# A decoder layer with two branches: another order of work in its first block

## The chip, the core and the metric

The kernel runs on one core of one Trainium2 chip. The metric is device time in microseconds (us), from the first to the last instruction of the program, as the median of several runs. TensorE (PE, with its weight loads as PEld) multiplies matrices into PSUM; VectorE (DVE), ScalarE (ACT) and GpSimd (POOL) work element by element; SyncE (SP) and ScalarE issue the transfers between HBM and SBUF.

## What is computed

One layer of a decoder over 16 meta tokens and 2048 tokens of 1024 channels. An input projection of the normalised input `u` feeds two branches, an SSD scan with a short convolution and a gated linear attention (GLA); their outputs are merged by sigmoid gates, projected, added to the input and normalised. Cut to what matters here:

```python
def hybrid_layer(hres, ...):
    u = rmsnorm(hres, norm_w)
    proj = jnp.einsum('bld,dn->bln', u, w_in)
    z, xbc, dt_raw, q, k, v, g_gla, a_lr, merge_g = split_cols(proj, IN_WIDTHS)
    xbc = jax.nn.silu(causal_depthwise_conv(xbc, conv_w, conv_b))
    ...
    dt = jax.nn.softplus((dt_raw + dt_bias).astype(jnp.float32))
    a = -jnp.exp(a_log.astype(jnp.float32))
    y_m, s_m = ssd_chunked(xs[:, :m], dt[:, :m], a, bm[:, :m], cm[:, :m], N_META, s0)
    y_r, _ = ssd_chunked(xs[:, m:], dt[:, m:], a, bm[:, m:], cm[:, m:], SSD_CHUNK, s_m)
    y = jnp.concatenate([y_m, y_r], axis=1) + d_skip[:, None] * xs
    y_ssd = rmsnorm_in_groups(y * jax.nn.silu(z), ssd_norm_w)
    gate_logit = jnp.einsum('blr,rk->blk', a_lr, gla_gate_w2) + gla_gate_b
    log_a = (jax.nn.log_sigmoid(gate_logit.astype(jnp.float32)) / GLA_GATE_TEMP)
    ... # GLA with q, k, v and the running sums of log_a; y_gla
    gates = jax.nn.sigmoid(merge_g)
    return hres + merged(gates, y_ssd, y_gla) @ w_out
```

## The kernel before

The 2048 tokens are four blocks of 512; block 0 also carries the 16 meta tokens (`m0` is 16 there and 0 elsewhere). Every product is made of three matmuls on TensorE, since each operand is split into a high half, rounded to the fast type, and a low half, the rest (`accum`, L209 to L211: high by high, high by low, low by high). The split of a weight is a copy on ScalarE and a subtraction on GpSimd (L171, L172); that of `u` a copy on ScalarE and a subtraction on VectorE (L336, L338). In block 0 each weight is loaded raw (L198), split, and stored split (L205), so that the later blocks load it ready. The raw weights have three buffers and the split ones four.

A block runs through pieces: `proj_zm` (the first quarter of z, the raw step sizes dt and the low-rank gate inputs), then convolution tiles and the other z, then q, k, v and output gates of the four GLA heads. The pieces are generators. Beside each step of the pieces, `step` moves every running helper on by one: the step-size chain (`dt_chain`), the GLA gates (`gates`), the SSD scan of a group (`ssd_scan`) and the GLA scan of a head. TensorE and SP take their instructions in the order of the code. For ScalarE, VectorE and GpSimd a scheduler sets the order when the program is built; `tc.issue_after(x)` holds the instructions made within it behind `x`. Each engine then takes its instructions strictly in its order.

The places that matter here, by the lines before:

- `load_u` for block 0 (L292 to L340): the mean square of each 128 rows, a power of -1/2 on GpSimd (L279), matmuls that spread it over the partitions (L317, L321), then for each of 8 tiles of channels the scaled `u` (L333, from a transfer L331), its high half (L336), a store (L337) and its low half (L338).
- four small scaled constants on VectorE (L356 to L362).
- `proj_zm` (L500 to L508): 8 weights of 288 columns; at its end the step-size chain is begun and z's four banks are evicted by `gate_z` (tanh on ScalarE, L494, and a product on VectorE, L495). The banks hold the raw step sizes and gate inputs too, which L413 and L414 take out.
- the first convolution tile (`proj_conv`, L563): two weights of 512 columns, halves 0 and 1 of the eight channel tiles.
- `late_constants`: the gates' second weight (L373 to L375) and masks (L377, L378), asked for beside the step after.
- `gates` (L453 to L487): for two heads at a time the logits on TensorE (L473), evicted by VectorE (L475) and ScalarE (L476), the log-sigmoid, and then for each head a subtraction (L483) and five running sums (L485: one of 16 columns, four of 128). In block 0 these stand behind the last convolution instruction (L573).
- `ssd_scan`: for each chunk of 128 tokens, `before` makes the masked decay `dm` (L650 to L653, the last a product on VectorE), and `after` multiplies with it (L662) and with the state, and reads the banks (L668 to L673).

## Time and profile before

| | |
|---|---|
| median of three runs | 2259.13 us (2258.09 to 2264.15) |
| the profiled execution, as a run | 2259.97 us |
| its span, first to last instruction | 2257.6 us |
| mean granted TensorE clock | 0.996 |
| DVE, ACT, POOL busy | 70%, 53%, 30% |
| HBM traffic | 228 GB/s over the span |

An engine's row in the page gives its busy time, its share of the span and the count of its instructions. A row of the timeline gives the start in us from the span's beginning, the duration in us, the engine (SPq and ACTq are the issuing of transfers), the line, the operation, the tile written and those read, the shapes, the count, and in brackets how long the engine had been idle just before and what ended it. A row of the waits gives who waited for whom, the sum in us, the times, and the longest. The granted clock is a share of TensorE's full speed.

### The profile page before, as it was taken

The page shows a single profiled execution, that of the slowest core. Times are in us where ns is not written, and L with a number is a line of the kernel's source. Part 1 is how long each engine was busy: PE and PEld are TensorE (multiplying, and loading weights), DVE is VectorE, ACT ScalarE, POOL GpSimd, SP SyncE. Part 2 cuts the span into 40 slices and gives each one's busy share as a digit, 9 for nine tenths or more (in the row PEclk, how much of TensorE's full clock was granted, in tenths as well). Part 3 has the DMA queues.
Part 4 walks back from the last instruction along what each step waited for, and adds up shares of the span by engine and source line. Part 5 has one row for each costly group of instructions (what it writes and reads, how often), then busy time and mean ns, then how long its engine had stood idle before and what let it go on. Part 6 is the DMA issues. An engine that isn't in the chain of part 4 may idle for free.

```text
span 2257.6 us, 34930 instructions
## 1 busy us (share of the span) xinstructions
PE 2217.3 (98%) x11789; PEld 1899.2 (84%) x11789; DVE 1575.8 (70%) x2935; ACT 1188.0 (53%) x2767; POOL 687.7 (30%) x681
## 2 busy tenths in 40 slices
PE   7999999999999999999999999999999999999998
PEld 6999989888888988888987888878888888888887
DVE  5776676677667676657677665684788855789966
ACT  4665655466445455544466454464644545554544
POOL 4344433222221122122122200066333264424341
PEclk9999999999999999999999999999999999999999
DMA  8666876667777666778666664376767866687753
GB/s 303 233 213 221 279 260 215 209 216 231 236 253 262 219 211 223 230 257 276 208 224 208 214 220 162 115 247 213 243 232 270 300 227 221 233 282 253 259 179 123
DMA packets 314210, 517.94 MB, mean 229 GB/s; under 512 B 28080, under 2 KB 162480, under 8 KB 314032
## 3 DMA queue, kind: packets, MB, share of 16 engines
q1 hardware_dynamic: 246864, 419.63, 56.6%
q10 hardware_dynamic: 67168, 96.10, 11.7%
q8 instruction: 92, 1.51, 0.3%
q14 instruction: 86, 0.70, 0.1%
HBM read 368.42 MB, written 147.19 MB: 228 GB/s over the span
## 4 chain that ended last, share of the span: by engine, by line
PE 88%; DVE 4%; ACT 3%; DMA 3%; issue 1%; POOL 1%; SPq 0%; ACTq 0%; POOLq 0%; DVEq 0%
PE pj L209 20%; PE pj L211 20%; PE pj L210 19%; PE pt L209 4%; PE pt L210 4%; PE pt L211 4%; PE pc L662 2%; PE pc L209 2%; PE pc L211 2%; PE pc L210 2%; PE pc L821 2%; PE pc L663 1%; PE pc L665 1%; PE pc L929 1%; DMA acc<-in_xmt 1%
## 5 line engine op out<-in xcount | busy, mean ns | idle before, releaser
L209 PE MATMUL pj<-ue,whl 128*128 128x264 f32 (+1 forms) x672 | 236.7, 352 | 3.9 <-ACT g_all L476 2.1
L211 PE MATMUL pj<-ue,whl 128*128 128x264 f32 (+1 forms) x672 | 231.1, 344 | 0.8 <-DVE tkc L421 0.8
L210 PE MATMUL pj<-ue,whl 128*128 128x264 f32 (+1 forms) x672 | 230.1, 342 | 0.0
L209 PE MATMUL pj<-uo,whl 128*128 128x512 f32 x512 | 205.7, 402 | 0.0
L211 PE MATMUL pj<-uo,whl 128*128 128x512 f32 x512 | 200.2, 391 | 0.0
L210 PE MATMUL pj<-uo,whl 128*128 128x512 f32 x512 | 199.4, 390 | 0.0
L209 PE MATMUL pj<-b,a 128*128 128x512 f32 (+1 forms) x484 | 188.7, 391 | 0.7 <-DVE io L1220 0.5
L210 PE MATMUL pj<-b,a 128*128 128x512 f32 (+1 forms) x484 | 187.7, 388 | 1.7 <-DVE b L1077 1.7
L211 PE MATMUL pj<-b,a 128*128 128x512 f32 (+1 forms) x484 | 188.9, 390 | 0.1
L573 DVE SCALAR_TENSOR_TENSOR acc<-cin,hcw,acc 128x512 f32<-128x512 f32 (+1 forms) x192 | 155.0, 807 | 42.2 <-ACT acc L569 41.1
L83 POOL TENSOR_TENSOR wr<-wr 128x256 f32<-128x256 f32 x80 | 66.9, 836 | 382.0 <-DMA wr<-u 159.1
L1102 DVE TENSOR_TENSOR a<-ar,a 128x512 fp32r<-128x512 f32 x160 | 132.8, 838 | 63.8 <-ACT a L1101 61.5
L1092 POOL TENSOR_TENSOR as<-ar,ar 128x512 f32<-128x512 f32 x40 | 62.1, 1553 | 376.9 <-DMA ar<-in_w_br 139.8
L209 PEld LDWEIGHTS pj<-ue,whl 128*128 128x128 f32 x672 | 127.7, 190 | 19.5 <-ACT g_all L476 2.3
L211 PEld LDWEIGHTS pj<-ue,whl 128*128 128x128 f32 x672 | 127.8, 190 | 15.9 <-POOL whl L172 1.0
L210 PEld LDWEIGHTS pj<-ue,whl 128*128 128x128 f32 x672 | 127.7, 190 | 14.8
L1077 DVE TENSOR_TENSOR b<-br,b 128x512 fp32r<-128x512 f32 x140 | 124.1, 909 | 22.3 <-ACT b L1076 21.7
L172 POOL TENSOR_TENSOR whl<-wr,whl 128x512 fp32r<-128x512 f32 (+1 forms) x76 | 97.1, 1286 | 134.4 <-ACT whl L171 95.1
L1102 DVE TENSOR_TENSOR a<-as,a 128x512 fp32r<-128x512 f32 x120 | 104.4, 871 | 44.3 <-ACT a L1101 42.0
L1136 ACT ACTIVATE sn<-pj 128x512 f32<-128x512 f32 x118 | 69.9, 593 | 118.5 <-PE pj L211 65.9
L1101 ACT ACTIVATE a<-ar 128x512 fp32r<-128x512 f32 x160 | 98.7, 624 | 55.8 <-PE pt L211 29.4
L1076 ACT ACTIVATE b<-br 128x512 fp32r<-128x512 f32 x140 | 85.9, 627 | 79.3 <-DMA br<-br_t 24.4
(328 smaller groups left out, 6500.2 us busy)
## 6 DMA issues: line engine op xcount, KB each, us to landing
whl<-k_s SPq DMA_DIRECT2D x96, 512.0 KB, 3.6
whl<-k_g SPq DMA_DIRECT2D x96, 512.0 KB, 4.1
whl<-k_v SPq DMA_DIRECT2D x36, 512.0 KB, 3.8
wr<-in_w_feat SPq DMA_DIRECT2D x64, 256.0 KB, 4.3
k_s<-whl SPq DMA_DIRECT2D x32, 512.0 KB, 3.7
cb<-cumd SPq DMA_DIRECT2D x64, 256.0 KB, 5.0
y<-gg ACTq DMA_DIRECT2D x64, 256.0 KB, 4.4
k_g<-whl SPq DMA_DIRECT2D x32, 512.0 KB, 3.8
```

The lines of the kernel that those rows point to most:

```text
L83: nc.gpsimd.tensor_tensor(o, x, y, op=ALU.subtract)
L172: nc.gpsimd.tensor_tensor(hl[:, 1], raw, hl[:, 0].bitcast(F32), op=ALU.subtract)
L209: nc.tensor.matmul(ps, sh, mh, start=first, stop=False, **kw)
L210: nc.tensor.matmul(ps, sh, ml, start=False, stop=False, **kw)
L211: nc.tensor.matmul(ps, sl, mh, start=False, stop=last, **kw)
L573: convd[:] = [nc.vector.scalar_tensor_tensor(acc, cin[:, k:k + tt], hcw[:, ti, k:k + 1], acc, op0=ALU.mult, op1=ALU.add)]
L1076: nc.scalar.activation(t[:, 0], raw, AF.Copy)
L1077: nc.vector.tensor_tensor(t[:, 1], raw, t[:, 0].bitcast(F32), op=ALU.subtract)
L1092: nc.gpsimd.tensor_tensor(s1, a21, a22, op=ALU.add)
L1101: nc.scalar.activation(t[:, 0], src, AF.Copy)
L1102: latest[:] = [nc.vector.tensor_tensor(t[:, 1], src, t[:, 0].bitcast(F32), op=ALU.subtract)]
L1136: nc.scalar.activation(sn, self.ps[n, "a"], AF.Copy)
```

## The change

Four things are put in another order, in block 0 alone; no arithmetic is changed.

1. In `load_u`, GpSimd's low half of z's first weight is held behind the power of the last rows; the scaling of channel tile `kt` is held behind the low half of tile `kt - 2`; the four scaled constants stand behind the low half of tile 1. (`rstd_rows` now also returns the power's instruction, for `first_rows`.)
2. In `proj_zm`, the two weights of the first convolution tile are loaded and split (`ready`) before the step-size chain is begun and z is evicted, and these stand behind the first split on ScalarE; the chain's first absolute value (L418) stands behind the second.
3. The gates' subtraction and running sums (`sums`) are put off to the end of each `step`.
4. There they stand behind the last of two kinds of instruction, the convolution's (as before) and now also the masks' product of `ssd_scan`.

```diff
+    ready, split_at, firsts = {}, [], []
+
     def load_w(key, src):
+        if key in ready:
+            return ready.pop(key)
         n = src.shape[-1]
...
-            nc.scalar.activation(hl[:, 0], raw, AF.Copy)
-            nc.gpsimd.tensor_tensor(hl[:, 1], raw, hl[:, 0].bitcast(F32), op=ALU.subtract)
+            split_at[:] = [nc.scalar.activation(hl[:, 0], raw, AF.Copy)]
+            with tc.issue_after(first_rows[0].ins) if key == "zm_0" else nullcontext():
+                nc.gpsimd.tensor_tensor(hl[:, 1], raw, hl[:, 0].bitcast(F32), op=ALU.subtract)
...
         if m0:
             rs.append(rm_s)
+            first_rows.append(rs[NCH - 1][1])
+            rs = [r for r, _ in rs]
...
+        lows = []
         for kt in range(KT):
...
-            for ps, a, n in rbs:
-                nc.vector.scalar_tensor_tensor(xk[:, a:a + n], xk[:, a:a + n], norm_w[:, kt:kt + 1], ps[:, :n],
-                                               op0=ALU.mult, op1=ALU.mult)
+            with tc.issue_after(lows[kt - 2].ins) if m0 and kt > 1 else nullcontext():
+                for ps, a, n in rbs:
+                    nc.vector.scalar_tensor_tensor(xk[:, a:a + n], xk[:, a:a + n], norm_w[:, kt:kt + 1], ps[:, :n],
+                                                   op0=ALU.mult, op1=ALU.mult)
...
-            nc.vector.tensor_tensor(u[kt][:, 1], xk, u[kt][:, 0].bitcast(F32), op=ALU.subtract)
+            lows.append(nc.vector.tensor_tensor(u[kt][:, 1], xk, u[kt][:, 0].bitcast(F32), op=ALU.subtract))
+            if m0:
+                first_low[:] = lows[:2][-1:]
...
+    scaled_consts = tc.issue_after(first_low[0].ins)
+    scaled_consts.__enter__()
     nc.vector.tensor_scalar(hcw, conv_w, 0.5, None, op0=ALU.mult)
...
+    scaled_consts.__exit__(None, None, None)
...
         e = wde[:, :nck]
-        nc.scalar.activation(e, x, AF.Abs)
+        with tc.issue_after(firsts[-1].ins) if m0 else nullcontext():
+            nc.scalar.activation(e, x, AF.Abs)
...
             for h in (h2, h2 + 1):
-                with tc.issue_after(convd[-1].ins) if m0 else nullcontext():
+                def sums(h=h):
                     nc.vector.tensor_tensor(gmt[:, h % 2, :tt], gmt[:, h % 2, :tt], g_all[:, h, :tt], op=ALU.subtract)
                     for a, n in chunks:
                         nc.vector.tensor_tensor_scan(g_all[:, h, a:a + n], ones[:, :n], gmt[:, h % 2, a:a + n], 0.0,
                                                      op0=ALU.mult, op1=ALU.add)
+
+                if m0:
+                    put_off.append(sums)
+                else:
+                    sums()
                 yield
...
-        begin(dt_chain(o, pss[NCH:] + pss[:NCH]))
-        for c, ps in enumerate(pss[:NCH]):
-            gate_z(zs[:, c], ps[:, :256])
+        if m0:
+            for i in range(2):
+                ready[f"s0_{i}"] = load_w(f"s0_{i}", w_feat[T_SSD, :, i * 512:(i + 1) * 512])
+                firsts.append(split_at[0])
+        with tc.issue_after(firsts[0].ins) if m0 else nullcontext():
+            begin(dt_chain(o, pss[NCH:] + pss[:NCH]))
+            for c, ps in enumerate(pss[:NCH]):
+                gate_z(zs[:, c], ps[:, :256])
...
-            nc.vector.tensor_tensor(dm, dm, scm[:, c].unsqueeze(1).to_broadcast([P, 4, P]), op=ALU.mult)
+            convd[:] = [nc.vector.tensor_tensor(dm, dm, scm[:, c].unsqueeze(1).to_broadcast([P, 4, P]), op=ALU.mult)]
...
             if next(gen, running) is running:
                 running.remove(gen)
+        while put_off:
+            with tc.issue_after(convd[-1].ins):
+                put_off.pop()()
```

In the changed program TensorE's order is the same from the first instruction to the last. The other engines' orders differ up to the first SSD scan, and are the same behind it. The line numbers grow by 4 at the weight split (L171 becomes L175) and by 25 at the scan (L653 becomes L678). Three places:

SP, behind z's last weight (`wr_537`). `act` and `tok` are the buffers of the gates' weight (`in_gw`) and the masks (`in_cmsk`), the transfers from `in_w_feat` the two weights of the first convolution tile, `k_zm` the stores of z's split weights. Before, and then in the changed order:

```order
L198 DMA wr_537<-in_w_zm 128x288
L373 DMA act_598<-in_gw 16x512 x3
L377 DMA tok_66_604<-in_cmsk 128x896
L205 DMA k_zm_497<-whl_491 256x1x288
L198 DMA wr_611<-in_w_feat 128x512
L205 DMA k_zm_534<-whl_528 256x1x288
L198 DMA wr_642<-in_w_feat 128x512
```

```order
L203 DMA wr_537<-in_w_zm 128x288
L210 DMA k_zm_497<-whl_491 256x1x288
L203 DMA wr_574<-in_w_feat 128x512
L210 DMA k_zm_534<-whl_528 256x1x288
L203 DMA wr_581<-in_w_feat 128x512
L387 DMA act_612<-in_gw 16x512 x3
L391 DMA tok_70_618<-in_cmsk 128x896
```

Both convolution weights now stand ahead of the gates' weight and the masks.

ScalarE at the end of z (`whl_535` is z's last weight; `pj_400` to `pc_404` are z's five banks, `alr` the gate inputs taken from them, `wde` the step-size chain, `w` the gates' weight). Before, the first convolution weight is `whl_609`; in the changed order the two are `whl_572` and `whl_579`, and `whl_699` is the next tile's:

```order
L171 ACTIVATE whl_535<-wr_537 128x288
L374 ACTIVATE w_387<-act_598 48x512
L494 ACTIVATE tok_46_399<-pj_400 128x256
L494 ACTIVATE tok_46_399<-pj_401 128x256
L414 ACTIVATE alr_398<-pj_400 128x48
L494 ACTIVATE tok_46_399<-pj_402 128x256
L414 ACTIVATE alr_398<-pj_401 128x48
L494 ACTIVATE tok_46_399<-pt_403 128x256
L414 ACTIVATE alr_398<-pj_402 128x48
L414 ACTIVATE alr_398<-pt_403 128x48
L414 ACTIVATE alr_398<-pc_404 128x48
L418 ACTIVATE wde_393<-ecu_394 128x80
```

```order
L175 ACTIVATE whl_572<-wr_574 128x512
L514 ACTIVATE tok_46_399<-pj_400 128x256
L514 ACTIVATE tok_46_399<-pj_401 128x256
L428 ACTIVATE alr_398<-pj_400 128x48
L175 ACTIVATE whl_579<-wr_581 128x512
L514 ACTIVATE tok_46_399<-pj_402 128x256
L388 ACTIVATE w_387<-act_612 48x512
L428 ACTIVATE alr_398<-pj_401 128x48
L514 ACTIVATE tok_46_399<-pt_403 128x256
L428 ACTIVATE alr_398<-pj_402 128x48
L428 ACTIVATE alr_398<-pc_404 128x48
L175 ACTIVATE whl_699<-wr_701 128x512
```

Before, `whl_609` followed the last of the rows shown. Now the first split stands ahead of z's evictions, the second among them, and the gates' weight between the evictions of the third and the row copy of the second bank.

VectorE in the first SSD scan, at the masks' product of the last chunk (`sq`, L653, later L678), with the convolution (`acc`), the silu (`act`), the second pair of heads' subtractions (`tok` from `g_all`) and running sums (`g_all`, named SCALAR_TENSOR_TENSOR with 16 or 128 columns here). Before, and then in the changed order:

```order
L573 SCALAR_TENSOR_TENSOR acc_1555<-cin_1554,hcw,acc_1555 128x528
L483 TENSOR_TENSOR tok_177_1434<-tok_177_1434,g_all_397 128x528 x2
L674 TENSOR_TENSOR c_209_1604<-c_209_1604,tok_132_1125 128x256
L653 TENSOR_TENSOR sq_1585<-sq_1585,sq_1123 128x512
L485 SCALAR_TENSOR_TENSOR g_all_397<-ones_r,tok_177_1434 128x16
L485 SCALAR_TENSOR_TENSOR g_all_397<-ones_r,tok_177_1434 128x128
L577 SCALAR_TENSOR_TENSOR act_1565<-act_1565,acc_1555 128x528
L485 SCALAR_TENSOR_TENSOR g_all_397<-ones_r,tok_177_1434 128x128 x3
```

```order
L598 SCALAR_TENSOR_TENSOR acc_1555<-cin_1554,hcw,acc_1555 128x528
L699 TENSOR_TENSOR c_209_1598<-c_209_1598,tok_132_1125 128x256
L678 TENSOR_TENSOR sq_1579<-sq_1579,sq_1123 128x512
L498 TENSOR_TENSOR tok_177_1434<-tok_177_1434,g_all_397 128x528 x2
L700 TENSOR_TENSOR tok_132_1125<-c_209_1598,tok_46_399 128x256
L602 SCALAR_TENSOR_TENSOR act_1565<-act_1565,acc_1555 128x528
L500 SCALAR_TENSOR_TENSOR g_all_397<-ones_r,tok_177_1434 128x16
L500 SCALAR_TENSOR_TENSOR g_all_397<-ones_r,tok_177_1434 128x128 x4
```

The masks' product comes ahead of the two subtractions, and all running sums of the pair behind the silu.

10 lines of the change are left out of this document (5 added, 5 removed).

## The prediction

> **What bounds the kernel now.** I read the page first, then TensorE's waits, then the windows around its gaps, then single instructions. From the page:
>
> ```profile
> span 2257.6 us, 34930 instructions
> PE 2217.3 (98%) x11789; PEld 1899.2 (84%) x11789; DVE 1575.8 (70%) x2935; ACT 1188.0 (53%) x2767; POOL 687.7 (30%) x681
> PE 88%; DVE 4%; ACT 3%; DMA 3%; issue 1%; POOL 1%; SPq 0%; ACTq 0%; POOLq 0%; DVEq 0%
> ```
>
> TensorE is busy for 98% of the span and holds 88% of the chain of waits. What can be won is its idle time, 2257.6 - 2217.3 = 40.3 us, and the time in which its clock runs low. TensorE's order is the same in both programs, and after about 135 us so is every other engine's. So only the waits of the first 150 us can change:
>
> ```profile
> PE pt L317 <- DMA cst<-in_cf: 10.1, 1, 10.1
> PE pc L662 <- DVE sq L653: 3.2, 1, 3.2
> PE pj L209 <- ACT g_all L476: 2.1, 1, 2.1
> PE pj L209 <- ACT whl L171: 1.6, 1, 1.6
> PE pj L211 <- DVE ue L338: 1.4, 1, 1.4
> PE pj L211 <- DVE tkc L421: 0.8, 1, 0.8
> PE pj L210 <- POOL whl L172: 0.5, 1, 0.5
> ```
>
> The first is the first transfer, which nothing here touches. The others are three places: the start (14 to 33 us), the gap between z and the first convolution tile (36 to 39 us), and two gaps beside the first SSD scan (at 105 and 122 us), which I call A and B. The windows show what each costs beyond its idle time. The columns are the stretch, its length, busy time of PE, PEld, DVE, ACT and POOL, the granted clock, the DMA share and GB/s:
>
> ```profile
> 35.20:38.60 3.40, 1.28 (x10) 0.97 (x8) 2.27 (x7) 2.53 (x8) 1.00 (x1) 1.00 0.37 127
> 38.60:42.00 3.40, 3.08 (x14) 3.08 (x15) 2.26 (x5) 1.69 (x4) 2.41 (x3) 0.50 0.66 213
> 103.50:106.90 3.40, 1.44 (x9) 1.13 (x8) 3.40 (x7) 0.41 (x2) 1.95 (x2) 0.99 0.77 229
> 106.90:110.30 3.40, 3.28 (x15) 3.28 (x16) 3.40 (x9) 3.40 (x11) 0.00 (x0) 0.50 0.01 2
> 120.50:123.90 3.40, 1.49 (x13) 1.28 (x11) 3.40 (x5) 1.88 (x5) 1.47 (x2) 1.00 0.42 139
> 123.90:130.70 6.80, 5.55 (x22) 5.19 (x23) 6.76 (x15) 0.41 (x2) 3.13 (x3) 0.50 0.86 272
> 861.20:864.60 3.40, 2.00 (x18) 1.73 (x15) 2.41 (x6) 3.37 (x7) 0.00 (x0) 1.00 0.76 233
> 864.60:868.00 3.40, 3.37 (x16) 2.83 (x17) 3.40 (x11) 3.27 (x11) 0.51 (x1) 1.00 0.99 356
> ```
>
> After a stretch of 3.4 us in which TensorE was busy for 1.28, 1.44 or 1.49 us, the next stretch is granted half the clock; after one with 2.00 us busy it is not. So a stretch must hold some 1.4 to 2.1 us of idle time for the clock to fall. Half of the busy time in a low stretch is lost: 3.08 / 2 = 1.54 us behind the gap at 36 us, 3.28 / 2 = 1.64 us behind A, 5.55 / 2 = 2.78 us behind B. [...]
>
> **The start** (the power ahead of the first weight split, the low half of u ahead of the later tiles, the four scaled constants behind). TensorE's first matmuls come up to 1.4 us earlier, the wait for L338. But z then waits for its last weight:
>
> ```profile
> 31.09 0.44 ACT L171 ACTIVATE whl<-wr 128x288 fp32r<-128x288 f32 x1 [3.03 <-DMA wr<-in_w_zm]
> 32.46 0.40 PE L210 MATMUL pj<-whl,ue 128*128 128x288 f32 x1 [0.48 <-POOL whl L172]
> ```
>
> ScalarE had been waiting 3.03 us for that transfer, and its place in SP's order is not changed. TensorE, started earlier, waits there longer. I take 0; the bounds are 0, and a gain of 1.4 us if the transfer lands earlier too.
>
> **The gap at 36 us** (two convolution weights loaded and split ahead of z's eviction).
>
> ```profile
> 35.70 0.26 PE L211 MATMUL pc<-whl,ue 128*128 128x32 f32 x1
> 37.58 0.39 PE L209 MATMUL pj<-ue,whl 128*128 128x264 f32 x1 [1.61 <-ACT whl L171]
> 38.92 0.59 PE L211 MATMUL pj<-ue,whl 128*128 128x264 f32 x1 [0.84 <-DVE tkc L421]
> 36.89 0.63 ACT L171 ACTIVATE whl<-wr 128x512 fp32r<-128x512 f32 x1
> 37.60 1.27 POOL L172 TENSOR_TENSOR whl<-wr,whl 128x512 fp32r<-128x512 f32 x1 [5.19 <-ACT whl L171]
> 26.58 1.37 SPq L373 DMA_DIRECT2D act<-in_gw  x3
> 30.18 0.61 SPq L198 DMA_DIRECT2D wr<-in_w_feat  x1
> 33.03 0.39 ACT L494 ACTIVATE tok<-pj 128x256 f32<-128x256 f32 x1 [0.82 <-PE pj L211]
> wr<-in_w_feat SPq DMA_DIRECT2D x6, 256.0 KB, 4.3
> ```
>
> TensorE is done with z at 35.96. The weight of the first convolution tile was issued at 30.18 and takes 4.3 us to land, so it lay there by 34.5, but ScalarE splits it only at 36.89, behind all of z's evictions, and GpSimd its low half at 37.60 to 38.87 (the second wait, put down to DVE L421, ends there too). In the changed order the gates' weight (three issues, 1.37 us) and the masks no longer stand ahead of it on SP, so it is issued at least 1.4 us earlier and lands by 33.1; its split (0.63 on ScalarE, then 1.27 on GpSimd) is done by 35.0, before TensorE asks at 35.96. z's evictions, which began at 33.03, begin at 33.7. By the order on ScalarE the second bank is free behind three evictions (0.39 each), the second split and the gates' weight (0.63 each), at 33.7 + 1.17 + 1.26 = 36.1 and a short row copy; TensorE comes to it three matmuls behind 35.96, at about 36.3. So both waits go, 1.61 + 0.84 us, and with them the low clock, 1.54 us: 3.99 us.
>
> What is queued behind the moved splits on ScalarE is the chain to the step sizes, which TensorE needs at L431:
>
> ```profile
> 40.02 1.21 DVE L428 TENSOR_TENSOR ecu<-tkd,nega 128x80 f32<-128x80 f32 x1
> 45.99 0.34 PE L431 MATMUL pt<-ecu,cst 128*128 128x80 f32 x2
> ```
>
> It was ready at 41.23 and used at 45.99. TensorE now comes to L431 at 45.99 - 3.99 = 42.00, and the chain, with one split more ahead of it (0.63 us), ends at about 41.9: no wait, but a cover of 4.8 us is gone. Bounds: from 0.8 us (the idle time becomes another wait of 1.6 us and the clock falls as before) to 3.99.
>
> That what comes behind can follow 4 us earlier rests on this row, since the transfers were pausing just there:
>
> ```profile
> 36.00:38.00 2.00, 0.42 (x2) 0.30 (x2) 0.87 (x5) 1.45 (x6) 0.40 (x1) 1.00 0.22 82
> ```
>
> **Gap A** (the first two heads' sums). Ahead of the gates' next evictions VectorE has the same instructions in both orders; only the masks' product (L653) and the silu (L577) change places with a subtraction and two scans. The end of the row moves only if these meet a GpSimd instruction differently:
>
> ```profile
> 101.65 1.72 DVE L577 SCALAR_TENSOR_TENSOR act<-act,acc 128x528 f32<-128x528 f32 x1
> 116.30 0.71 DVE L577 SCALAR_TENSOR_TENSOR act<-act,acc 128x528 f32<-128x528 f32 x1 [3.22 <-ACT act L576]
> ```
>
> The same L577 takes 1.72 us with a GpSimd split beside it and 0.71 without, so such a meeting costs 1.0 us. I take 0 for A, with bounds of one meeting either way (-1.0 to +1.0).
>
> **Gap B** (the sums of heads 2 and 3 put behind the masks).
>
> ```profile
> 121.77 1.31 DVE L483 TENSOR_TENSOR tok<-tok,g_all 128x528 f32<-128x528 f32 x2
> 123.35 1.75 DVE L653 TENSOR_TENSOR sq<-sq,sq 128x512 f32<-128x512 f32 x1
> 100.29 0.68 DVE L653 TENSOR_TENSOR sq<-sq,sq 128x512 f32<-128x512 f32 x1
> 123.22 3.01 POOL L172 TENSOR_TENSOR whl<-wr,whl 128x512 fp32r<-128x512 f32 x2 [1.93 <-ACT whl L171]
> ```
>
> TensorE stopped at 121.99 for L653, which stood behind two subtractions (1.31 us, less the overlap of 0.07 us: 1.24) and then met the GpSimd split that had begun at 123.22, so that it took 1.75 us in place of 0.68. Without the subtractions it starts at 123.35 - 1.24 = 122.1 and ends at 122.8, before that split begins. It is ready 125.1 - 122.8 = 2.3 us earlier, and some 0.8 us of idle time are left. That is too little for the clock to fall: another 2.78 us. What is late next is VectorE itself. It still has the subtractions and ten scans to do before it reads the bank that TensorE wants at L621:
>
> ```profile
> 130.56 0.42 DVE L673 TENSOR_TENSOR c<-c,pc 128x256 f32<-128x256 f32 x1
> 135.65 1.06 PE L621 MATMUL pc<-act,act 128*128 128x128 f32 x8
> ```
>
> TensorE now arrives at 135.65 - 2.3 - 2.78 = 130.6; the read ended at 130.98. So 0.4 us go back, and B gives 2.3 + 2.78 - 0.4 = 4.7 us. Bounds: 0.8 us (one more meeting of 1.07 us ahead of L653, and the clock still falls) to 5.1 us.
>
> **The sum**: 0 + 3.99 + 0 + 4.7 = 8.7 us. The span becomes 2257.6 - 8.7 = 2248.9. The profiled execution took 2259.97 us as a run, 0.84 above the median of 2259.13, so the median run should be 2259.13 - 8.7 = 2250.4 us.
>
> **Rivals.** (1) *The idle time goes, the low clock comes back.* The low stretches lie on a grid of 3.4 us that the kernel does not set: a gap A of 2.1 us, or what is left of B, can fall into one stretch and cost two stretches again. For it: 1.49 us busy was enough. Against it: what is left of B is 0.8 us, and nothing is left at 36 us. Then only idle time is won: 1.61 + 0.84 + 2.3 - 0.4 = 4.35, giving 2254.8.
>
> (2) *The gap at 36 us is given back.* ScalarE takes its instructions in order, and z's evictions, the row copies and the step-size chain now wait behind two weight transfers and the gates' weight. If these land 2 us later than 4.3 us after issue, TensorE waits for a bank or at L431 instead; or the weights behind cannot follow. For it: the cover of 4.8 us is gone. Against it: the queue had a share of 0.22. Gain 4.7: 2254.4.
>
> (3) *Slower: the sums meet GpSimd.* All twelve instructions of the put-off sums stand ahead of the read that frees TensorE's bank at L621, and they now start where two splits run (123.22 to 126.2). [...] Each meeting costs 1.07 us directly, and with two of them the 2.78 us of clock are lost again. From six meetings more than before (6.4 + 2.78 against 8.7) the kernel is slower; with eight (8.6 + 2.78) it is 2.7 us slower: 2261.8. Against it: GpSimd is busy for 3.13 of 6.8 us there, which is room for three meetings, and those of before (L653's among them) are already in the sum.
>
> **How the numbers follow.** Forecast 0.60, rival 1 0.17, rival 2 0.15, rival 3 0.08. A measurement of this kernel can tell about 0.3%, 6.8 us, from no change, so faster means below 2252.4. The forecast's own range is 2247 to 2253, of which most is below that: 0.53, and 0.03 from rivals 1 and 2 with a gain at the start; 0.56 faster. Rivals 1 and 2 otherwise (0.29), the forecast's upper end (0.07) and the nearer part of rival 3 (0.05) are within 0.3%: 0.41. Slower by more takes twelve meetings: 0.03. The range that should hold the time is 2246.5 (the better bounds of the start, A and B together, 2.8 us, and 1.1 us of spread) to 2257.0 (past rivals 1 and 2).
>
> **What would show it.** Right: no wait of TensorE for the split of `whl` near 36 us and a granted clock of 1.00 from 36 to 42 us; L653 of the third chunk ending some 2.3 us before the second pair of sums would have let it; the clock at 1.00 behind B. Wrong: a wait at L431 or for a bank near 36 us; the clock at 0.50 behind B; a wait at L621 of more than 1 us; the wait for `g_all` at A over 3 us.

## The result and the profile after

| | before | changed |
|---|---|---|
| median of the runs made side by side | 2260.81 us (2258.09 to 2264.15, 8 runs) | 2254.55 us (2251.84 to 2257.45, 8 runs) |
| the profiled execution, as a run | 2259.97 us | 2251.84 us |
| its span | 2257.6 us | 2249.8 us |

The ratio is 0.9969 with an interval of 0.9960 to 0.9978: 5 to 9 us faster. Three executions of the sets below, which took 2745 to 5068 us, are left out of medians and ratios. The profiled executions lie 7.8 us apart in span, the medians 6.3 us. The forecast was a gain of 8.7 us and a time of 2250.4 us.

The page of the changed kernel, with the span, the engines' busy time and the chain of waits:

```profile
span 2249.8 us, 34929 instructions
PE 2214.2 (98%) x11789; PEld 1895.6 (84%) x11789; DVE 1577.9 (70%) x2935; ACT 1188.9 (53%) x2767; POOL 686.4 (31%) x681
PE 86%; DVE 5%; ACT 4%; DMA 3%; issue 2%; POOL 1%; SPq 0%; ACTq 0%; POOLq 0%; DVEq 0%
```

TensorE's busy time fell by 3.1 us, from 2217.3, with the same 11789 matmuls; the forecast had 1.54 + 2.78 = 4.32 us of low clock to win. Its idle time fell by 4.7 us, from 40.3 to 35.6, where the forecast had 4.35.

Five of TensorE's waits of the first 150 us in the changed kernel (who waited for whom; sum in us, times, longest):

```profile
PE pj L214 <- ACT g_all L491: 2.1, 1, 2.1
PE pc L687 <- DVE sq L678: 0.8, 1, 0.8
PE pj L214 <- ACT alr L428: 0.7, 1, 0.7
PE pt L446 <- DVE ecu L443: 0.6, 1, 0.6
PE pc L646 <- DVE c L698: 0.3, 1, 0.3
```

The waits for the convolution weight (1.6 us) and for `tkc` (0.8) are gone, and B fell from 3.2 us to 0.8. A is as it was, 2.1 us. New are 0.7 us for z's second bank, 0.6 us at the first matmul of the step sizes (L446, before L431), and 0.3 us at L646 (before L621). At the start the wait of 1.4 us for a low half of `u` (L338) is gone, and the two waits for its high halves (L336, now L345) are 2.2 us in place of 1.7.

The stretches of the changed kernel that answer to those of before (busy time of PE, PEld, DVE, ACT and POOL, then the granted clock, the transfers' share and GB/s):

```profile
38.00:42.00 4.00, 3.35 (x27) 3.06 (x26) 1.82 (x6) 3.94 (x10) 2.08 (x2) 1.00 0.94 355
99.40:102.80 3.40, 1.38 (x8) 1.06 (x7) 3.40 (x7) 0.44 (x2) 1.61 (x2) 1.00 0.72 231
102.80:106.20 3.40, 3.31 (x15) 3.31 (x16) 3.40 (x9) 3.40 (x11) 0.00 (x0) 0.51 0.00 0
117.00:120.40 3.40, 2.60 (x21) 2.32 (x19) 3.40 (x5) 1.78 (x4) 1.47 (x3) 1.00 0.64 196
120.40:127.00 6.60, 6.36 (x53) 6.00 (x51) 6.57 (x16) 2.27 (x5) 3.01 (x4) 1.00 0.80 258
```

Only the stretch behind A is still at half the clock; the one near 38 us and the two behind B are at 1.00.

Where the time went can be read from four instructions of TensorE that stand in every version, in the same order: the end of z (the last matmul into `pc`), the first matmul of the step sizes, the last logits of heads 2 and 3 (the second pair of heads; the last instruction ahead of A but for the scan's), and the first scores of the second SSD group (behind B). For the changed kernel these rows are:

```profile
33.71 0.26 PE L216 MATMUL pc<-whl,ue 128*128 128x32 f32 x1
41.50 0.45 PE L446 MATMUL pt<-ecu,cst 128*128 128x80 f32 x2 [0.65 <-DVE ecu L443]
97.90 0.28 PE L488 MATMUL pt<-act,w 48*128 48x264 f32 x1
127.07 0.46 PE L646 MATMUL pc<-act,act 128*128 128x128 f32 x2 [0.31 <-DVE c L698]
```

The same four in the profiled execution of every kernel that ran, and the three distances between them (us; the first column is the end of the row, the others its start):

| kernel | z ends | step sizes | logits | scores | z to sizes | sizes to logits | logits to scores |
|---|---|---|---|---|---|---|---|
| before | 35.96 | 45.99 | 102.07 | 135.65 | 10.03 | 56.08 | 33.58 |
| before, again | 35.56 | 44.22 | 105.42 | 138.16 | 8.66 | 61.20 | 32.74 |
| changed | 33.97 | 41.50 | 97.90 | 127.07 | 7.53 | 56.40 | 29.17 |
| changed, again | 33.53 | 40.90 | 97.07 | 126.25 | 7.37 | 56.17 | 29.18 |
| changed, third | 33.71 | 40.94 | 97.34 | 129.25 | 7.23 | 56.40 | 31.91 |
| start alone | 33.62 | 44.67 | 100.46 | 133.08 | 11.05 | 55.79 | 32.62 |
| weights alone | 35.46 | 41.76 | 98.14 | 130.75 | 6.30 | 56.38 | 32.61 |
| sums alone | 35.72 | 44.37 | 105.50 | 134.67 | 8.65 | 61.13 | 29.17 |
| constants later | 34.43 | 42.35 | 99.36 | 129.71 | 7.92 | 57.01 | 30.35 |
| second head later | 33.87 | 41.55 | 98.25 | 123.53 | 7.68 | 56.70 | 25.28 |
| both later | 34.73 | 42.12 | 99.09 | 123.25 | 7.39 | 56.97 | 24.16 |
| zero matmuls at A | 33.52 | 42.76 | 101.59 | 130.72 | 9.24 | 58.83 | 29.13 |
| constants behind ln | 33.95 | 40.04 | 97.39 | 126.58 | 6.09 | 57.35 | 29.19 |
| ln and second head | 33.64 | 39.77 | 97.49 | 122.79 | 6.13 | 57.72 | 25.30 |

In the first pair of profiles the change has won 4.49 us at the step sizes and 8.58 at the scores. What is left at the end is 7.8.

### The profile page after: what moved, and what is told of

Same layout as the page of the kernel before. It is cut to its first block, busy times and chain, and to the rows that moved or that the text cites. A ratio compares the mean times of both kernels' runs of the same rounds, so it can differ in the third digit from the quotient of the medians.

```text
span 2249.8 us, 34929 instructions
## 1 busy us (share of the span) xinstructions
PE 2214.2 (98%) x11789; PEld 1895.6 (84%) x11789; DVE 1577.9 (70%) x2935; ACT 1188.9 (53%) x2767; POOL 686.4 (31%) x681
## 3 DMA queue, kind: packets, MB, share of 16 engines
q8 instruction: 92, 1.51, 0.3%
## 4 chain that ended last, share of the span: by engine, by line
PE 86%; DVE 5%; ACT 4%; DMA 3%; issue 2%; POOL 1%; SPq 0%; ACTq 0%; POOLq 0%; DVEq 0%
PE pj L214 19%; PE pj L216 19%; PE pj L215 19%; PE pt L214 4%; PE pt L215 4%; PE pt L216 4%; PE pc L214 2%; PE pc L216 2%; PE pc L215 2%; PE pc L687 2%; PE pc L846 2%; PE pc L688 1%; PE pc L690 1%; PE pc L954 1%; PE pt L662 1%
## 5 line engine op out<-in xcount | busy, mean ns | idle before, releaser
L215 PE MATMUL pt<-b,a 128*128 128x512 f32 x320 | 125.4, 392 | 0.1
```

Source lines behind the costliest of these rows:

```text
L215: nc.tensor.matmul(ps, sh, ml, start=False, stop=False, **kw)
```

## The experiments

Times are medians; "before" is the kernel before, run beside them on the same chip.

| kernel | us | before | ratio and interval |
|---|---|---|---|
| start alone | 2260.08 | 2261.71 | 0.9991 (0.9982 to 1.0000) |
| weights alone | 2256.92 | 2261.71 | 0.9973 (0.9963 to 0.9984) |
| sums alone | 2258.96 | 2261.71 | 0.9986 (0.9977 to 0.9995) |
| changed, again | 2254.99 | 2261.71 | 0.9961 (0.9947 to 0.9975) |
| before, again | 2260.37 | 2261.02 | 0.9996 (0.9988 to 1.0005) |
| constants later | 2254.65 | 2261.02 | 0.9966 (0.9954 to 0.9978) |
| second head later | 2249.68 | 2261.02 | 0.9943 (0.9931 to 0.9955) |
| both later | 2247.58 | 2261.02 | 0.9938 (0.9925 to 0.9952) |
| zero matmuls at A | 2257.39 | 2261.61 | 0.9982 (0.9974 to 0.9991) |
| constants behind ln | 2251.96 | 2261.61 | 0.9957 (0.9943 to 0.9970) |
| ln and second head | 2247.66 | 2261.61 | 0.9936 (0.9923 to 0.9948) |
| changed, third | 2254.11 | 2260.24 | 0.9972 (0.9961 to 0.9983) |

**The start alone.** The change without its parts 2 to 4:

```diff
...
-                if m0:
-                    put_off.append(sums)
-                else:
+                with tc.issue_after(convd[-1].ins) if m0 else nullcontext():
                     sums()
...
-        if m0:
-            for i in range(2):
-                ready[f"s0_{i}"] = load_w(f"s0_{i}", w_feat[T_SSD, :, i * 512:(i + 1) * 512])
-                firsts.append(split_at[0])
...
```

Expected:

> The first part alone (the power and the low halves held at the start; the convolution weights and the sums as before). In the trace of the changed kernel z ended 1.5 us earlier than before, and its last weight landed 2.3 us earlier. Theory: the 1.5 us come from this part, and are then swallowed by the first convolution tile, whose weight split on ScalarE still stands behind z's evictions: the time is 0 to 1.5 us below the kernel before, with z ending at about 34.5 us and the gap behind it 1.6 us or longer. Rival: the earlier end comes from run to run differences of the weights' landing; then z ends at about 36 us here and the time is that of before.

z ended at 33.62 us, 2.3 us earlier than in the first profile of before. The earlier end comes from this part and is not chance: in the table z ends at 35.46 to 35.96 us in the four executions without the part, and at 33.52 to 34.73 in the ten with it. The time fell by 1.6 us, at the edge of what the interval tells. Of the 2.3 us, 1.3 are left at the step sizes (44.67 us against 45.99), and none against the second profile of before (44.22). The first convolution weight is still split behind z's evictions, and in this execution the clock then fell for two stretches:

```profile
35.10:38.51 3.41, 2.74 (x11) 2.43 (x11) 2.76 (x5) 2.83 (x6) 2.26 (x2) 0.50 0.39 145
38.51:41.93 3.42, 3.42 (x17) 3.42 (x17) 0.39 (x1) 0.63 (x1) 1.53 (x2) 0.50 0.95 270
```

**The weights alone.** The change with only part 2 (the low halves, constants and sums as before). Expected:

> The second part alone (the first two convolution weights issued and split ahead of z's evictions). Theory (idle time and clock go together): the wait for the split of whl near 36 us goes, the granted clock stays at 1.00 from 38.6 to 42.0 us, and 3 to 4 us are won; gap A and gap B stay as they were (2.1 and 3.2 us), with the clock at 0.5 behind both. Rival (the clock is not the cause): only the idle time goes, at most 2.4 us.

Measured 4.8 us by the medians. The windows view of this kernel, near the end of z and behind B:

```profile
38.60:42.00 3.40, 3.04 (x26) 2.82 (x24) 1.80 (x5) 3.34 (x9) 1.82 (x2) 1.00 0.92 363
118.09:121.50 3.41, 0.34 (x4) 0.28 (x3) 3.41 (x5) 1.64 (x4) 2.21 (x2) 1.00 0.80 232
121.50:124.91 3.41, 3.41 (x14) 3.05 (x14) 3.41 (x8) 0.00 (x0) 1.41 (x2) 0.50 0.87 266
```

The clock near 38 us stays at 1.00, and the step sizes come at 41.76, which is 4.23 us earlier than before. The idle time and the low stretch went together here (the wait of 1.6 us is gone, the clock is 1.00), as the theory had it, and the interval (3.6 to 8.4 us) leaves out the rival's 2.4. But behind B, which is as it was (3.1 us), only one stretch is low, where before had two; the stretch after 124.91 us is granted 1.00. It is the first sign that the clock's share is not a property of the kernel.

**The sums alone.** The change with only parts 3 and 4. Expected:

> The third and fourth parts alone (the gates' sums put off behind each step's masks; start and weights as before). Theory: gap B shrinks from 3.2 us to about 0.8, the granted clock behind it is 1.00 for the 6.8 us in which it was 0.5, and 4.4 to 4.7 us are won; the gap at 36 us and its low clock stay. Rival (the clock falls behind gap B all the same, since the grid of its windows has moved): 1.9 us are won. With the parts adding up, start, weights and sums together give the 6 to 8 us of the whole change.

The medians fell by 2.75 us, between theory and rival. From logits to scores takes 29.17 us in place of 33.58, as in the whole change: 4.4 us, as expected. But near 36 us this execution went another way than the first profile of before. The waits of this kernel, and two of its stretches:

```profile
PE pj L213 <- ACT acc L588: 2.8, 2, 2.6
PE pj L213 <- ACT whl L175: 1.6, 1, 1.6
36.82:40.23 3.41, 2.06 (x14) 1.85 (x15) 2.38 (x5) 3.21 (x6) 1.88 (x2) 1.00 0.23 94
47.06:50.47 3.41, 2.06 (x9) 2.06 (x10) 0.77 (x1) 3.39 (x7) 2.17 (x3) 0.50 0.77 295
50.47:53.88 3.41, 3.41 (x18) 3.41 (x17) 1.87 (x5) 1.51 (x5) 0.56 (x1) 0.50 0.95 299
```

The 1.6 us wait for the weight is there, yet the clock does not fall behind it (1.00 from 36.82 to 40.23, and 8.65 us from z's end to the step sizes in place of 10.03). TensorE so comes 1.6 us sooner to the next weights, waits 2.6 us for an eviction that stands behind a weight's transfer on ScalarE, and there the clock falls for two stretches. From sizes to logits takes 61.13 us in place of 56.08.

**The changed kernel again.** No edit. Expected:

> The changed kernel once more, beside its parts on the same chip. Theory: 6 to 8 us below the kernel before, with the low clock only behind gap A, as in its first profile. Rival (the clock stretches fall elsewhere from one execution to the next): other low stretches in this profile, each with some 1.5 us more of span.

The same waits at A and B as in its first profile (2.1 and 0.8 us), from logits to scores 29.18 us in place of 29.17, and the same mean granted clock, 0.998; 6.7 us below before by the medians. The parts' medians add up to 1.6 + 4.8 + 2.75 = 9.2 us. The interval of each is some 2 us or more either way, so that the whole gives less is not shown by the times. It would fit the table: the start brings z's end 2 us forward, but with the weights moved too the step sizes come only 0.3 to 0.9 us earlier than with the weights alone.

**The kernel before again.** No edit. Expected:

> The kernel before once more, nothing changed. Theory (the grid of the granted clock lies differently from one execution to the next, and a gap of TensorE costs no, one or two stretches of 3.4 us by where it falls): gaps of 1.6, 2.1 and 3.1 us as in the first profile, but low stretches at other distances behind them; the time from the first matmul of the gates of heads 2 and 3 to L621 is 32.6 us with one low stretch behind gap B, or 33.6 with two, as first seen. Rival (the stretches hang on the kernel alone): 1, 1 and 2 low stretches again. The medians of the two sets of runs differ by no more than 2 us in either case.

Its windows: the gap at 36 us and what follows it, A, and B.

```profile
36.82:40.23 3.41, 2.22 (x16) 2.02 (x17) 2.55 (x5) 3.05 (x6) 2.04 (x2) 1.00 0.29 114
43.65:47.06 3.41, 2.02 (x16) 1.70 (x14) 0.24 (x1) 0.73 (x3) 1.27 (x1) 1.00 0.95 354
47.06:50.47 3.41, 2.63 (x12) 2.63 (x13) 0.77 (x1) 3.38 (x7) 2.73 (x3) 0.50 0.86 318
125.57:128.98 3.41, 0.34 (x3) 0.34 (x4) 3.41 (x5) 1.58 (x4) 2.27 (x2) 1.00 0.81 240
128.98:132.40 3.42, 3.42 (x14) 3.06 (x14) 3.42 (x9) 0.00 (x0) 1.41 (x2) 0.50 0.91 267
```

The same program with nearly the same gaps (1.6, 2.2 and 3.1 us) has no low stretch at 38 us, two at 47 us behind a wait of 2.2 us that the first profile does not have, and one behind B in place of two. The theory holds and its rival falls: the low stretches begin at 38.60, 106.86 and 123.93 us in the first profile, and at 47.06, 111.92 and 128.98 here. In both traces the changes of the clock lie 3.41 us or multiples of it apart (3.41, 64.85, 3.41, 13.65 and 6.83 us in the first; 6.82, 58.04, 3.41, 13.65 and 3.42 here), and this grid lies differently in the two: from 38.60 to 47.06 is 8.46 us, 2.48 times 3.41.

**The constants later.** The changed kernel, with the gates' weight, the masks and the third convolution weight's split held behind the step-size chain:

```diff
+            with tc.issue_after(steps[0].ins) if key == "s1_0" else nullcontext():
+                split_at[:] = [nc.scalar.activation(hl[:, 0], raw, AF.Copy)]
...
+        with tc.issue_after(steps[0].ins):
+            nc.scalar.activation(w2, w2r, AF.Copy)
...
-        nc.scalar.activation(e, e, AF.Exp, scale=-1.0)
+        done = nc.scalar.activation(e, e, AF.Exp, scale=-1.0)
...
-        nc.vector.tensor_tensor(x, dt, nega.unsqueeze(1).to_broadcast([P, nck, NH]), op=ALU.mult)
+        steps[:] = [done, nc.vector.tensor_tensor(x, dt, nega.unsqueeze(1).to_broadcast([P, nck, NH]), op=ALU.mult)]
```

Expected:

> The changed kernel with the gates' weight, the masks and the split of the third convolution weight (s1_0) held behind the step-size chain on ScalarE and VectorE. Theory: the two waits that the change left near 36 us go, 0.5 to 0.7 us for the second bank (behind the gates' weight) down to under 0.2, and 0.65 to 0.67 us at the first matmul of the step sizes down to 0; that matmul comes 1.0 to 1.3 us earlier than in the changed kernel (measured from the end of z) and the time is some 1 us below the changed kernel's. Rival: the wait goes on to the third convolution weight, whose split now comes later; then nothing is won.

The wait for the bank went (0.2 us), the one for the step sizes grew to 1.3. Neither theory nor rival had the cause, which stands in ScalarE's timeline:

```profile
39.26 0.63 ACT L176 ACTIVATE whl<-wr 128x512 fp32r<-128x512 f32 x1 [1.59 <-DMA k_s<-whl]
41.20 0.27 ACT L442 ACTIVATE dec<-tkc 128x80 f32<-128x80 f32 x1
```

The third weight's split waits not for its own transfer but for the store of an older split weight, whose buffer it needs (`k_s` from `whl`). Held behind the exponential, it still stands ahead of the logarithm (L442), which now waits with it. The time is that of the changed kernel.

In this execution A (2.1 us) fell across two stretches (2.08 and 2.64 us busy of 3.41), and the clock stayed at 1.00 there. TensorE came to B 1.2 us earlier, counted from the logits, and waited 2.0 us in place of 0.8, and the clock fell there instead (0.50 from 120.65 to 124.06, behind a stretch with 1.41 us busy).

**The second head later.** The changed kernel, with the second head's sums held until the evictions of heads 2 and 3 are emitted, so that these come first on VectorE:

```diff
+            put_off.extend(held)
+            held.clear()
...
-                if m0:
+                if m0 and h == 1:
+                    held.append(sums)
+                elif m0:
                     put_off.append(sums)
```

Expected:

> The changed kernel with the sums of the second head (one subtraction and five scans) held until the evictions of heads 2 and 3 have been emitted. Theory: VectorE reads the gates' banks 3 us earlier, gap A (2.1 us) goes, with it the low stretch behind it (1.4 to 1.7 us): 3.5 to 3.8 us below the changed kernel, no low stretch left before the end. Rival: the held sums are in the way ahead of gap B, where the third chunk's masks or the scans make TensorE wait as it did before; then B is 2 us or longer and less than 1.5 us is won.

TensorE's largest wait of this kernel between 90 and 150 us, which is B, and VectorE's first read of the banks at A:

```profile
PE pc L692 <- DVE sq L683: 0.7, 1, 0.7
98.84 0.48 DVE L491 TENSOR_SCALAR tok<-pj,pv 128x264 f32<-128x264 f32 x1
```

The read came at 101.84 in the changed kernel. No wait for the gates' eviction is left, and the granted clock is 1.00 from 98 to 106 us and from 114 to 122 us, and 0.999 over the execution. From logits to scores takes 25.28 us, 3.9 less than 29.17, and the time fell by 4.9 us against the changed kernel's first median. The theory holds for the wait at A. Its second reason, the low stretch behind A, does not: the zero matmuls below take that stretch away and win nothing by it.

**Both edits.** Expected:

> Both edits together. Theory: they touch different stretches (33 to 41 us, 95 to 103 us) and add up: 4.5 to 5 us below the changed kernel, 11 to 12 below the kernel before, with the clock at 1.00 from about 21 us to the end. Rival: TensorE comes earlier to the transfers behind, and half of it is given back before 300 us.

2247.58 us: 7.0 below the changed kernel's first median, 13.4 below before, more than expected. The wait for the step sizes (1.5 us) came with the edit of the constants.

**Zero matmuls at A.** The changed kernel, with 15 matmuls of a zero weight into the bank just being filled (the zero tile and the list `filler` are made at the start):

```diff
+                    for _ in range(filler.pop() if filler else 0):
+                        nc.tensor.matmul(ps[:, :n], zero_r, moving(kt, a, n)[0], start=False, stop=False)
...
+            if m0 and h2 == 2:
+                filler.append(15)
```

Expected:

> The changed kernel with 15 further matmuls (264 columns each, a zero weight, into the bank that is being filled) put into TensorE's queue just where it waits in gap A. They fill the 2.1 us in which it was idle and take part in no result. Theory of the clock: the low stretch behind A goes, since TensorE was busy; from the end of A to the start of B takes 13.8 us in place of 15.0. Theory of the pace: VectorE sets the time from A to B, so what the clock gives is lost again as a longer wait at B (2.0 us in place of 0.8, as in the run with the constants later, where A fell without a low stretch); L646 comes no more than 0.3 us earlier, and the time is that of the changed kernel. Rival (the clock is worth its 1.2 us to the end): B stays at 0.8 us, L646 comes 1.2 us earlier.

The windows of this kernel behind A, and its wait at B:

```profile
104.00:107.40 3.40, 3.09 (x25) 2.88 (x24) 3.40 (x9) 1.33 (x4) 0.71 (x2) 1.00 0.54 150
107.40:110.80 3.40, 3.40 (x30) 3.40 (x29) 3.40 (x9) 3.40 (x10) 0.00 (x0) 1.00 0.12 35
PE pc L696 <- DVE sq L687: 2.0, 1, 2.0
```

The clock stays at 1.00, B's wait is 2.0 us, and from logits to scores takes 29.13 us in place of 29.17. So what the clock gives at A is lost as a wait at B, to 0.04 us. The same stands in the other traces: from the logits to the matmul that waits at B takes 20.81 to 20.86 us here, in the three executions of the changed kernel and with the constants later, whether the clock fell behind A or not. Who sets the pace there is seen in the chain of waits, six pieces of it, here of the changed kernel (start, length, what):

```profile
98.84 2.76 DVE g_all L500 x5
101.92 0.42 DVE tok L490
102.36 1.68 ACT g_all L491 x4
108.56 1.09 ACT g_all L494
116.30 1.43 DVE acc L598
118.06 0.60 DVE sq L678
```

From A to the masks that end B the chain runs over VectorE and ScalarE (the gates' evictions and log-sigmoid, then the convolution), and not once over TensorE. The theory named VectorE alone; it is the two. The time, though, is 2.8 us above the changed kernel's, which no theory had. In this trace the loss lies ahead of A: a wait of 2.8 us for the step sizes, and 58.83 us from sizes to logits in place of 56.40, at a mean granted clock of 0.997 in place of 0.998. The two rows that bear on it are the last product of the step-size chain and GpSimd's split, in this kernel and then in the changed one:

```profile
41.36 1.34 DVE L450 TENSOR_TENSOR ecu<-tkd,nega 128x80 f32<-128x80 f32 x1
41.34 1.26 POOL L182 TENSOR_TENSOR whl<-wr,whl 128x512 fp32r<-128x512 f32 x1 [1.38 <-ACT whl L180]
41.21 0.24 DVE L443 TENSOR_TENSOR ecu<-tkd,nega 128x80 f32<-128x80 f32 x1
41.22 1.35 POOL L177 TENSOR_TENSOR whl<-wr,whl 128x512 fp32r<-128x512 f32 x1 [1.37 <-ACT whl L175]
```

The same product took 1.34 us where it started 0.02 us behind the split, and 0.24 where it started 0.01 us ahead of it. That is 1.1 us of the 2.15 by which the wait grew. Whether the added zero tile causes it in all of this kernel's executions is open.

**The constants behind the logarithm.** As the constants later, one instruction further on:

```diff
-        done = nc.scalar.activation(e, e, AF.Exp, scale=-1.0)
+        nc.scalar.activation(e, e, AF.Exp, scale=-1.0)
...
-        nc.scalar.activation(ln, w1, AF.Ln)
+        done = nc.scalar.activation(ln, w1, AF.Ln)
```

Expected:

> As the run with the constants later, but the third weight's split held behind the logarithm (one instruction further on), so that its buffer, which comes free only when the copy of an older weight has gone out, no longer holds up the logarithm. Theory: the step sizes are ready by 38.5 us, the wait at the first matmul of the step sizes (1.3 to 1.5 us there, 0.65 in the changed kernel) goes to 0, and it comes 6.2 to 6.4 us behind the end of z (6.9 to 7.1 in the changed kernel). Time: 1 us below the changed kernel or the same within the spread. Rival: the wait passes on to the evictions of the first convolution tile, with the third weight's split before them; then a wait of 0.8 us or more near 50 us takes back what was won.

The step sizes are used at 40.04, 6.09 us behind z, with no wait; then this:

```profile
47.61 0.63 ACT L176 ACTIVATE whl<-wr 128x512 fp32r<-128x512 f32 x1 [1.45 <-DMA wr<-in_w_feat]
49.03 0.39 PE L215 MATMUL pj<-ue,whl 128*128 128x264 f32 x1 [1.29 <-ACT acc L598]
```

Theory and rival are both right in part: 1.4 us are won at the step sizes and 0.9 to 1.0 given back by the logits, because ScalarE then waits for a weight's transfer ahead of an eviction. The median, 2251.96, is 2.6 us below the changed kernel's; the trace accounts for 0.5 of that at the scores (126.58 against 127.07), since it stands beside the fastest of the changed kernel's first eight executions.

**The logarithm and the second head.** Both of the last edits. Expected:

> The constants behind the logarithm together with the second head's sums later. Theory: 1 us below the run with the second head later (2249.7), no low stretch before the end. Rival: what is won near 40 us is taken back by VectorE ahead of gaps A and B, so the time is that of the run with both edits (2248.4) within the spread.

2247.66 us: 2.0 us below the second head later, and as long as both edits (2247.58), from which five runs of 2245.4 to 2248.3 us cannot tell it. The mean granted clock is 0.999, in place of 0.998; from sizes to logits 57.72 us in place of 56.40, so that, as the rival had it, 1.3 us of what was won near 40 us are given back by 98 us. Against before it is 0.9936 (0.9923 to 0.9948), about twice the gain of the change.

**The changed kernel a third time.** No edit. Expected:

> The changed kernel a third time, for the trace of another execution: both of its traces so far are of the fastest execution of their sets (2251.8 and 2249.9 us, with medians of 2254.6 and 2255.0). Theory (a race on GpSimd's side): where the last subtraction of the step-size chain (L443) starts just after GpSimd's split of the weight behind it, it takes 1.3 us in place of 0.24, the wait at the first matmul of the step sizes grows from 0.65 us to 1.7 us or more, and the clock may fall behind it for two stretches; such an execution is 3 to 5 us longer than 2250. Rival (the executions above 2254 us lose their time behind 300 us, in transfers): then this trace stands within 1 us of the first two up to L646, whatever its time.

This execution took 2253.88 us, close to its median of 2254.11. Both theories fall. The chain's last product (L443, called a subtraction above) was not caught (0.24 us) and the wait for the step sizes is 0.7 us as in the other two; but the trace stands 2.2 to 3.0 us behind them at the scores already. Its windows at A and B:

```profile
97.75:101.16 3.41, 2.46 (x18) 2.15 (x16) 3.41 (x6) 0.57 (x2) 2.75 (x4) 1.00 0.47 154
101.16:104.57 3.41, 2.19 (x18) 2.19 (x19) 3.41 (x9) 2.72 (x8) 0.00 (x0) 1.00 0.27 77
114.81:118.22 3.41, 1.42 (x13) 1.21 (x12) 3.41 (x6) 2.14 (x6) 1.28 (x1) 1.00 0.16 53
118.23:121.64 3.41, 3.41 (x13) 3.14 (x13) 3.41 (x3) 0.79 (x2) 3.06 (x3) 0.50 0.95 295
121.64:125.05 3.41, 3.41 (x17) 3.32 (x17) 3.41 (x11) 0.51 (x2) 0.69 (x1) 0.50 0.78 195
```

A, with 2.2 us of idle time as ever, lies across two stretches (2.46 and 2.19 us busy), and the clock stays at 1.00. TensorE therefore comes early to B, waits 2.0 us there, and now the clock falls to 0.50 for two stretches. From logits to scores takes 31.91 us, 2.74 more than in the first profile. So the forecast's first rival, that the low clock comes back behind what is left of B, is true of this execution and not of the other two (29.17 and 29.18 us).

## Why the prediction was right, and where it was off

**The direction and the two places were right.** The two places named are those where the time was won, each shown by the part that was made alone. What the prediction counted for the low clock fits the first pair of profiles, but is not a fixed property of the two kernels.

**The start: forecast 0, with a better bound of 1.4 us; measured 2.0 to 2.4 us at z's end.** The step that failed is that TensorE, started earlier, would only wait the longer for z's last weight. In the changed kernel ScalarE split this weight at 28.82 in place of 31.09, after waiting 1.29 us in place of 3.03, and TensorE did not wait for it:

```profile
28.82 0.45 ACT L175 ACTIVATE whl<-wr 128x288 fp32r<-128x288 f32 x1 [1.29 <-DMA wr<-in_w_zm]
```

But the late weight belongs to one execution of before and not to its order. In the kernel before, run again, it was split at 29.41 us and TensorE waited for it nowhere, and yet z ended at 35.56 us, only 0.40 us sooner than in the first profile. So the weight holds up z's end by no more than the 0.48 us of the prediction's own row. What goes with the part is TensorE's wait of 1.4 us for a low half of `u` (L338): it is in all four executions without the part and in none of the ten with it. The two together are 1.9 us; where the rest comes from is open. What the earlier end is worth at the step sizes is 0.3 to 0.9 us, against the weights alone, since ScalarE's chain does not follow. The forecast of nearly nothing held for the time by luck, by another way than argued.

**The gap at 36 us: forecast 3.99; with the weights alone 4.23 at the step sizes.** The idle time (1.61 + 0.84) went, and the low stretch with it. That the two numbers lie so close is in part chance, since it is taken against the first profile of before. The second has no low stretch here, and against it the step sizes come 2.46 us earlier, which is the idle time alone; that trace then loses its time near 47 us. From z's end to the logits, the weights alone take 62.68 us, against 66.11 and 69.86 in the two. Two statements under it were wrong in the whole change, where z ends 2 us earlier: the second bank, said to be free before TensorE asks, is 0.7 us late, because the gates' weight (L388) stands ahead of the row copy; and the chain to the step sizes, said to be in time, is 0.65 us late. Both are among the signs of being wrong that the prediction named. The cover of 4.8 us that it gave up was indeed needed. It counted one split more ahead of the chain; three stand there now, at 31.98, 33.56 and 37.85 us, where before one stood, at 36.89. The third of them was not in the forecast. It waits for a store that frees its buffer, and the chain stands behind it:

```profile
37.85 0.63 ACT L175 ACTIVATE whl<-wr 128x512 fp32r<-128x512 f32 x1 [2.34 <-DMA k_s<-whl]
```

**Gap A: forecast 0; measured 0** (2.08 us before, 2.11 after).

**Gap B: forecast 4.7; measured 4.41 in the first pair of profiles.** The left-over wait of 0.8 us and the 0.3 to 0.4 us at L646 came out as worked out. The term that was mis-sized is the clock. The 2.78 us were read from an execution in which B lay across two stretches. The old B section costs 33.58 us with two low stretches and 32.6 to 32.7 with one (three of its four traces). The changed one costs 29.17 where the clock falls behind A, and 31.91 where it falls behind B instead, for two stretches (30.35 with one, in the run with the constants later). By these traces the gain of this place is anything from 32.6 - 31.91 = 0.7 to 33.58 - 29.17 = 4.4 us. That the first pair shows the largest of these, close to the forecast, is luck.

**The total.** In the first pair of profiles 8.58 us had been won at the scores, against the 8.7 of the sum; 7.96 were left at TensorE's 1000th instruction (152.05 us in place of 160.01), 7.4 at its 3000th (448.69 in place of 456.08) and 7.8 at the end. But the changed kernel's first profile is the fastest of its eight executions, and the third one, with 6.4 us won at the scores and 6.1 at the end, is nearer to the median. That trace lacks 8.7 - 6.1 = 2.6 us of the forecast, and the course with the clock low behind B costs 2.74. The median's gain lacks 2.4. The other 1.7 us between 2250.4 and 2254.55 are the basis: the median of before was 2259.13 in three runs and 2260.81 in eight. The measured median lies inside the range of 2246.5 to 2257.0, but outside the 2247 to 2253 that the prediction called the forecast's own. It lies beside the times of rivals 1 and 2 (2254.8 and 2254.4), so the time alone does not tell the forecast from them. The traces tell more: near 38 us the clock is 1.00 in the first profile of the changed kernel, and the other two took no longer there (7.53, 7.37 and 7.23 us from z's end to the step sizes, 10.03 before), which rival 1 did not have; behind B it fell, to 0.50, in the third. How often each course is taken is not known; only profiled executions show it, and there are three of the changed kernel.

**The rivals.** The first came true at B in one of three traces. The second was there in small: ScalarE's order cost 1.3 us of new waits, not 4. The meetings of the third took place in the scan, but no more of them than before. In the changed kernel's first profile, beside GpSimd's two splits (119.09 to 122.12 us), the two subtractions take 2.40 us in place of 1.31 and a product behind them (L700) 1.51 in place of 0.40; before it was L653 (1.75 against 0.68) and the first two running sums (1.58 against 0.50). Such a meeting was also seen at the step sizes, in the kernel with zero matmuls (1.34 us in place of 0.24).

## What to carry to other kernels

Ask of a stretch over which engines the chain of waits runs, before counting another engine's lost clock: behind A, TensorE's half clock cost nothing (29.17 us from logits to scores with it, 29.13 without), because VectorE and ScalarE set the pace, and putting 3.5 us of VectorE's work (a subtraction of 0.70 us and a head's five sums, 2.84) behind A won 4.9 us, as much as the largest of the change's parts. Take the price of a gap's low clock from several traces of the same program, since one trace shows only one of the ways in which the gap can lie (33.58 and 32.74 us for the same section in the two of before). And before an instruction is put ahead of a chain on an in-order engine, look for the buffer that it needs as well as for its own transfer: the third split here waited 2.34 us for one, with the chain behind it.

## What the hardware did that was not expected

**The clock does not follow the busy time alone.** The prediction put the limit between 1.49 and 2.00 us busy of 3.4 (so 1.4 to 1.9 us of idle time, where it wrote 1.4 to 2.1). In the kernel before, run again, the clock fell behind a stretch with 2.02 us busy (the row at 43.65 above), and with the sums alone behind one of 2.17 us; with the weights alone it did not fall behind one of 1.66 us:

```profile
1490.23:1493.64 3.41, 1.66 (x6) 1.05 (x6) 3.41 (x3) 1.89 (x3) 3.40 (x3) 1.00 0.41 145
1493.64:1497.05 3.41, 2.82 (x12) 2.35 (x13) 3.41 (x6) 0.66 (x2) 0.00 (x0) 1.00 0.52 153
```

The matmuls differ (512 columns there, 264 and some of 16 to 80 near 45 us), but what decides was not tried. How long the clock stays low is as open. Behind four stretches at half the clock with TensorE busy throughout (at 127.34 in before, 128.98 in before again, 123.85 in the start alone and 121.50 in the weights alone, 3.41 or 3.42 us each) it was 1.00 again, and one with 2.63 us busy (47.06) was followed by another low one. But in the changed kernel's third execution the stretch at 118.23, with 3.41 us busy, was followed by another low one too.

**Three hundredths of a microsecond lay between 0.24 us and 1.34.** VectorE's product of 128x80 that ends the step-size chain took 0.24 us where it started 0.01 us ahead of a GpSimd split (in the three executions of the changed kernel, with the constants later and with both edits), and 1.34 in the kernel with zero matmuls, where it started 0.02 us behind the start of one and ended 0.10 us behind its end. In the first profile of before it started 0.16 us behind the start of one and took 1.21. What holds it up there was not tried.
